# The first feed-forward of a decoder layer, rebuilt in two phases with seven block products

## The chip, the cores and the metric

The kernel runs on one core of a Trainium2 chip. The core has a matrix engine (TensorE, PE in the profile; its weight loads are PEld), three engines for elementwise work (VectorE or DVE, ScalarE or ACT, GpSimd or POOL), a SyncE (SP) that only issues transfers, and 16 DMA engines that move data between DRAM and the on-chip memory SBUF. Matmul results land in PSUM banks, from which DVE or ACT fetch them. Each engine runs its own instructions in order and waits for the others by semaphores.

The metric is the device time of one execution in microseconds (us), lower is better. A difference of about 0.3% is what a measurement of this kernel can tell from none.

## The reference

One decoder layer on a sequence of 1024 tokens of width 1024, in float32: a half-weighted feed-forward, a mixer (attention heads beside state-space heads), cross-attention on 256 memory tokens, and a second half-weighted feed-forward, each between two root-mean-square norms.

```python
def swiglu(h, w_gu, w_down):
    gu = h @ w_gu                      # 1024 x 5632
    g, u = jnp.split(gu, 2, axis=-1)   # two of 2816
    return (jax.nn.silu(g) * u) @ w_down

def reference(x, mem, ...):
    h = x
    f = swiglu(rmsnorm(h, ffn1_pre_g), ffn1_w_gu, ffn1_w_down)
    h = h + 0.5 * rmsnorm(f, ffn1_post_g)
    m = hybrid_mixer(rmsnorm(h, mix_pre_g), w_in, ..., w_out)
    h = h + rmsnorm(m, mix_post_g)
    c = memory_cross_attention(rmsnorm(h, xa_pre_g), rmsnorm(mem, mem_g), xa_wq, xa_wkv, xa_wo)
    h = h + rmsnorm(c, xa_post_g)
    f = swiglu(rmsnorm(h, ffn2_pre_g), ffn2_w_gu, ffn2_w_down)
    return h + 0.5 * rmsnorm(f, ffn2_post_g)
```

The change touches the first feed-forward, and what is prepared during it for later stages.

## The kernel before

**Numbers.** A float32 matrix is written as a high and a low part in the engine's fast float format: `split` (lines 245 to 249) casts the high part on ACT and subtracts it from the source on DVE (or on POOL, if asked). A product is then three matmuls: high by high, high by low, low by high (`mm3`, line 264).

**Tiling.** Activations lie transposed, 128 features by 512 tokens to a tile: 8 depth tiles for each half of the sequence (`XH`, `XL`; hh is 0 or 1). A gate or up weight tile is 128 output columns by 8 depths (512 KB). One projection of one weight tile and one half is 8 x 3 = 24 matmuls of 512 columns (`proj`, line 271). The inner width of 2816 gives 22 hidden tiles, each with a gate weight and an up weight.

**Order of work.** PE's order is written out by hand: each matmul is chained to the one before it, and a clock adds a modelled cost for each (0.422 ns a column, line 130). Work for other engines that should happen beside the matmuls is put on a list with a due time on that clock (`self.later`) and is issued when the clock gets there (`run_later`).

**First feed-forward** (`ffn1`, line 579). For each hidden tile it projects gate and up for both halves; DVE applies the norm's row (line 588), ACT the silu, DVE multiplies in the up result (line 593), and the product is split into high and low on ACT and POOL and kept in SBUF (line 596). After each two hidden tiles follow their down products (`down`, line 470): 96 matmuls into the `dn` banks, added into 16 running sums F by DVE (line 499). At the end, half 0 gets its last down products first; then its norm and residual (`post`, line 378) run beside half 1's last gate, up and down products. Half 1's norm runs beside the start of the state-space stage (`ssd`).

**Prepared weights** (`prepare`, line 185; `prepare_all`, line 226). During the first feed-forward, 82 weight tiles of later stages are loaded, split on ACT and DVE, and written back to DRAM as high and low parts: 20 of the state-space stage, 24 of attention, 16 of the mixer's output ("out"), 8 query and 8 output weights of cross-attention ("q", "o"), and 6 of the second feed-forward. One half of a tile is one step, due every 3500 on the clock from 40000. A stage takes a weight by `wtile` (line 169): a prepared one as two loads of 512 KB, another as one load of 512 KB and a split on the spot. `wstream` keeps one weight ahead.

**Second feed-forward** (`ffn2`, line 655), in two phases. `up_phase` (line 689) does the first three hidden tiles plainly (PLAIN). For the other 19 it sees the weights and the inputs as 2 x 2 blocks (depth halves by gate and up; depth halves by sequence halves) and needs seven block products of 12 matmuls instead of eight (`seven`, line 805). For this it makes sums of input blocks (S1, S4, S5, and differences that overwrite parts of XH and XL; `combine`, line 722), sums of weight blocks on POOL (line 773), and combines the results on DVE, ACT and POOL. Hidden results go to DRAM (`store`, line 701). `down_phase` (line 861) then loads them again, together with the down weights, three loads ahead.

Of the kernel before, what the change touches and what calls it, by code (L numbers as in the profile page):

```python
# [46 lines left out]
class Kern:  # L47
# [137 lines left out]
    def prepare(self, tiles, sp, t0, step):  # L185

# [275 lines left out]
    def dtile(self, src):  # L462
        raw = self.t(self.dp, [P, H], F32, "draw", bufs=2)
        self.nc.sync.dma_start(out=raw, in_=src)
        wh = self.t(self.dp, [P, H], F32R, "dhi", bufs=4)
        wl = self.t(self.dp, [P, H], F32R, "dlo", bufs=4)
        self.split(wh, wl, raw)
        return wh, wl

    def down(self, blocks, halves, first):  # L470


        for dh in range(2):
            ws = [self.dtile(src[dh, k]) for src, _ in blocks for k in range(2)]
            for hh in halves:
                ps = [self.t(self.dnp, [P, H], F32, "dn", bufs=4) for _ in range(4)]
                for j, w in enumerate(ws):
                    for i in range(4):
                        self.down_mm(ps[i], w, blocks[j // 2][1][(j % 2, hh)], i, hh, j == 0, j == len(ws) - 1)
                        if j == len(ws) - 1:  # L480
                            self.down_sum(self.F[hh][self.fi(dh, i, hh)], ps[i], first)

# [93 lines left out]
    def new_F(self):  # L576
        self.F = [[self.t(self.fp, [P, H], F32, f"F{hh}{d}") for d in range(KT)] for hh in range(2)]

    def ffn1(self, wgu, wdn, gpost, gnext, begin):
        nc = self.nc  # L580
        with self.pools("ff", ["a"], ["f"]) as (sp, fp, dnp):
            self.fp, self.dp, self.dnp, self.rows = fp, fp, dnp, False
            self.new_F()
            NB = NFF // 2

            def gate(ps, hh):
                t = self.t(sp, [P, H], F32, "ft", bufs=2)
                nc.vector.tensor_tensor(out=t, in0=ps, in1=self.R[hh], op=ALU.mult)  # L588
                nc.scalar.activation(t, t, AF.Silu)
                return t  # L590

            def up(t, ps):
                nc.vector.tensor_tensor(out=t, in0=t, in1=ps, op=ALU.mult)  # L593
                hi = self.t(sp, [P, H], F32R, "hhi", bufs=7)
                lo = self.t(sp, [P, H], F32R, "hlo", bufs=7)
                self.split(hi, lo, t, nc.gpsimd)
                return hi, lo

            def one(f, hh, act):
                t = gate(self.proj_now(next(W), hh), hh)  # L600
                act[(f, hh)] = up(t, self.proj_now(next(W), hh))

            def both(f, act):
                w = next(W)
                ts = [gate(self.proj_now(w, hh), hh) for hh in range(2)]
                w = next(W)
                for hh in range(2):
                    act[(f, hh)] = up(ts[hh], self.proj_now(w, hh))

            idx = list(range(4 * NB))
            idx += idx[-4:]
            W = [wgu[i] for i in idx]
            act = {}
            w = [self.wtile(W[0])]
            begin(0)
            w.append(self.wtile(W[1]))
            begin(1)
            w.append(self.wtile(W[2]))  # L620
            begin(2)
            ts = []
            for hh in range(2):
                t = gate(self.proj_now(w[0], hh), hh)
                act[(0, hh)] = up(t, self.proj_now(w[1], hh))
                ts.append(gate(self.proj_now(w[2], hh), hh))
            self.prepare_all(sp)
            W = self.wstream(W[3:])
            w = next(W)
            for hh in range(2):  # L630
                act[(1, hh)] = up(ts[hh], self.proj_now(w, hh))
            for b in range(1, NB - 1):
                prev, act = act, {}
                both(0, act)
                self.down([(wdn[b - 1], prev)], [0, 1], b == 1)
                both(1, act)
            prev = act
            act = {}
            one(0, 0, act)
            one(1, 0, act)  # L640
            last = [(wdn[NB - 2], prev), (wdn[NB - 1], act)]
            self.resid(0, 2000)
            self.down(last, [0], False)
            self.run_later(float("inf"))
            self.post(0, gpost, self.C[0], gnext, step=1800)
            one(0, 1, act)
            one(1, 1, act)
            self.place(fp, 32)
            self.resid(1, 2000, 6000)
            self.down(last, [1], False)  # L650
            c1 = self.C[1]
            self.flush(0)
            self.post(1, gpost, c1, gnext)

    def ffn2(self, wgu, wdn, gpre, gpost, out):
# [4 lines left out]
        nc, tc = self.nc, self.tc  # L660
        NB = NFF // 2
        with self.pools("f2", ["r"], []) as (rw, dnp):
            self.dnp, self.rows = dnp, True
            act_d = [[tc.dram_tile([P, 2, H], F32, name=f"act{b}{hh}") for hh in range(2)] for b in range(NB)]
            self.banks = self.raws = 0
            plain = [self.wsrc("gu2", i) for i in range(2 * PLAIN)]

            def bank():
                self.banks += 1
                if self.banks % 7 < 3:  # L670
                    return self.t(self.mmp, [P, H], F32, "mm")
                return self.t(dnp, [P, H], F32, "dn", bufs=4)

            def load(src, shape):
                self.raws += 1
                pool, tag = ((self.wp, "wraw"), (rw, "raw2"))[self.raws // 2 % 2]
                raw = self.t(pool, shape, F32, tag, bufs=2)
                nc.sync.dma_start(out=raw, in_=src)
                return raw

            with tc.tile_pool(name=self.nm("up"), bufs=1, reuse_waits="tile") as sp, \
                    tc.tile_pool(name=self.nm("ub"), bufs=1, reuse_waits="tile") as sp2:
                self.up_phase(sp, sp2, wgu, gpre, act_d, bank, load, plain)
            with tc.tile_pool(name=self.nm("dl"), bufs=1, reuse_waits="tile") as sp, \
                    tc.tile_pool(name=self.nm("dr"), bufs=1, reuse_waits="tile", side="right") as fp:
                self.fp, self.ep = fp, sp
                self.down_phase(sp, wdn, act_d, bank, load, gpost, out)

    def up_phase(self, sp, sp2, wgu, gpre, act_d, bank, load, plain):
        nc = self.nc  # L690

        fts, es = [self.t(sp, [P, H], F32, "ft", bufs=4)], [self.t(sp, [P, H], F32, "e")]
        S = {n: [self.t(sp, [P, 2, H], F32R, f"S{n}{k}") for k in range(4)] for n in (1, 4, 5)}
        S = {n: [(x[:, 0], x[:, 1]) for x in v] for n, v in S.items()}
# [3 lines left out]
        def ft():  # L698
            return fts.pop() if fts else self.t(sp, [P, H], F32, "ft", bufs=4)
# [14 lines left out]
        def tiles(n, src):  # L714
            tmp[n] = self.t(sp2, [P, 2, H], F32, "blk", bufs=5)
            for i, (hh, d) in enumerate(src):
                self.kp(nc.gpsimd.dma_start(out=tmp[n][:, i], in_=self.h[hh][d]))
# [4 lines left out]
        def combine(dst, x, d, y, op):  # L722

            u = self.t(sp, [P, 4, P], F32, "wc", bufs=3).rearrange("p a b -> p (a b)")
# [24 lines left out]

        def again(k):  # L750
# [11 lines left out]
        def pieces(f):  # L762
# [4 lines left out]
            for a, b, op in (  # L767
# [3 lines left out]
                if b is not None:  # L771
                    t = self.t(sp, [P, 4, P], F32, "wc", bufs=3)
                    nc.gpsimd.tensor_tensor(out=t, in0=a, in1=b, op=op)
                    a = t
                n = self.nblk = (self.nblk + 1) % 11
# [1280 lines left out]
```

## Time and profile before

| What | Value |
|---|---|
| median of 3 runs | 2861.12 us |
| lowest, highest run | 2856.28, 2863.88 us |
| the profiled execution, its own time | 2858.9 us |
| mean granted TensorE clock of the profiled execution | 0.981 |

The profile is of one execution. Its span runs from the first to the last instruction and is 1.8 us shorter than that execution's time; all stretches below are counted from the start of the span. By the instructions in the trace, the first feed-forward's products end at 750 us, the state-space stage follows to about 1128, attention to about 1733, the mixer's output to about 1905, cross-attention to about 2155, and the second feed-forward to the end.

In a row of a stretch stand the busy times of the engines, the clock that PE was granted, and the share of time in which the DMA engines were at work. In a row of a group stand the line, the engine, the operation, what it writes and reads, how often, the busy time and the mean length of one, and the idle time of the engine just before them with what ended it.

### The profile page before, as it was taken

The numbers are of one execution on the slowest core, as the hardware profiler recorded it, in microseconds if no ns is written. First come the engines' busy times: TensorE is split into PE (matmuls) and PEld (weight loads), VectorE is DVE, ScalarE is ACT, GpSimd is POOL, SyncE is SP. The second block draws the span as 40 slices with busy tenths as digits, with TensorE's granted clock in tenths as the row PEclk, the third lists the DMA queues.
The fourth block names the chain that finished last, engine by engine and source line by source line (L and its number), as shares of the span: only waits on it lengthen the run. The fifth ranks groups of instructions, "written<-read, shape, count | busy, mean of one in ns | idle before, by whom it ended". The sixth has DMA issues, their size and how long they took to land.

```text
span 2857.1 us, 36755 instructions
## 1 busy us (share of the span) xinstructions
PE 2748.1 (96%) x13194; PEld 2249.0 (79%) x13194; DVE 1769.7 (62%) x2590; ACT 1242.7 (43%) x2213; POOL 716.3 (25%) x862
## 2 busy tenths in 40 slices
PE   8999999999899999999999899999999999999998
PEld 7888888888677778888888787787777688888887
DVE  5555555556766565778777885636255855555657
ACT  6333333334444454566666663324344433332223
POOL 2010000002513343000000042432123655543322
PEclk9999999999899999999999999999999999999999
DMA  5788777876422224343333437666457322224332
GB/s 186 252 271 272 260 258 268 264 252 207 166 89 74 74 72 153 113 115 101 89 90 96 130 123 271 230 219 208 173 206 260 127 75 88 89 81 140 129 132 101
DMA packets 195734, 464.63 MB, mean 163 GB/s; under 512 B 23520, under 2 KB 32608, under 8 KB 195552
## 3 DMA queue, kind: packets, MB, share of 16 engines
q1 hardware_dynamic: 105184, 277.70, 29.8%
q10 hardware_dynamic: 77184, 140.54, 14.6%
q0 software_dynamic: 13184, 44.05, 4.4%
q8 instruction: 104, 1.70, 0.2%
q14 instruction: 78, 0.64, 0.1%
HBM read 314.35 MB, written 126.88 MB: 154 GB/s over the span
## 4 chain that ended last, share of the span: by engine, by line
PE 82%; DVE 8%; ACT 4%; issue 3%; DMA 2%; POOL 1%; SPq 0%; DVEq 0%; ACTq 0%; POOLq 0%
PE mm L133 50%; PE dn L133 24%; DVE nb L1468 2%; PE z L133 2%; PE tr L136 1%; PE ms L133 1%; DVE be L1472 1%; PE ms L136 1%; PE y L133 1%; ACT nb L1463 1%; PE seg L133 1%; DMA wlo<-dwlo 1%; ACT be L1463 1%; DVE acc L359 1%; DVE xl L256 1%
## 5 line engine op out<-in xcount | busy, mean ns | idle before, releaser
L133 PE MATMUL mm<-xh,whi 128*128 128x512 f32 x1776 | 720.5, 408 | 19.3 <-ACT xh L253 8.8
L133 PE MATMUL mm<-xl,whi 128*128 128x512 f32 (+1 forms) x1768 | 697.5, 395 | 3.6 <-DVE xl L256 2.0
L133 PE MATMUL mm<-xh,wlo 128*128 128x512 f32 x1768 | 694.2, 395 | 0.0
L133 PEld LDWEIGHTS mm<-xh,whi 128*128 128x128 f32 x1776 | 338.9, 191 | 84.2 <-ACT xh L253 9.6
L133 PEld LDWEIGHTS mm<-xh,wlo 128*128 128x128 f32 x1768 | 336.3, 190 | 75.1 <-issue 1.4
L133 PEld LDWEIGHTS mm<-xl,whi 128*128 128x128 f32 x1768 | 337.8, 191 | 60.8 <-DVE xl L256 3.7
L248 POOL TENSOR_TENSOR hlo<-ft,hhi 128x512 fp32r<-128x512 f32 x44 | 68.7, 1561 | 580.5 <-ACT hhi L246 580.5
L1468 DVE TENSOR_TENSOR_SCAN nb<-nb,begin 128x128 f32<-128x128 f32 (+7 forms) x128 | 176.4, 1381 | 33.6 <-ACT nb L1463 33.6
L499 DVE TENSOR_TENSOR F<-F,dn 128x512 f32<-128x512 f32 (+1 forms) x221 | 146.3, 682 | 78.1 <-PE dn L133 78.1
L133 PE MATMUL dn<-hhi,dhi 128*128 128x512 f32 x352 | 138.5, 393 | 3.9 <-DVE F L499 3.9
L133 PE MATMUL dn<-hlo,dhi 128*128 128x512 f32 x352 | 138.8, 394 | 0.0
L133 PE MATMUL dn<-hhi,dlo 128*128 128x512 f32 x352 | 138.3, 393 | 0.0
L1463 ACT ACTIVATE nb<-z,scale 128x128 f32<-128x128 f32 (+2 forms) x192 | 111.8, 582 | 41.9 <-PE z L133 40.1
L246 ACT CAST whi<-wraw 128x1024 fp32r<-128x1024 f32 (+1 forms) x83 | 78.8, 950 | 77.3 <-PE dn L133 30.9
L1463 ACT ACTIVATE be<-z,scale 128x128 f32<-128x128 f32 (+2 forms) x192 | 111.1, 579 | 0.0
L1472 DVE TENSOR_TENSOR be<-be,nb 128x128 f32<-128x128 f32 (+7 forms) x128 | 103.8, 813 | 11.5 <-DVE nb L1468 0.5
L1467 POOL MEMSET nb<- 128x1 f32 x128 | 12.7, 99 | 385.0 <-DVE be L1472 362.6
L359 POOL TENSOR_TENSOR acc<-acc,sq 128x512 f32<-128x512 f32 x45 | 62.3, 1384 | 144.8 <-ACT sq L357 144.7
L588 DVE TENSOR_TENSOR ft<-mm,rpre 128x512 f32<-128x512 f32 x44 | 30.4, 691 | 98.3 <-PE mm L133 96.4
L359 DVE TENSOR_TENSOR acc<-acc,sq 128x512 f32<-128x512 f32 x45 | 45.4, 1009 | 72.0 <-ACT sq L357 71.5
L133 PE MATMUL mm<-ath,v 128*128 128x256 f32 x320 | 87.9, 297 | 1.9 <-ACT sq L1483 1.9
L593 DVE TENSOR_TENSOR ft<-ft,mm 128x512 f32<-128x512 f32 x44 | 30.3, 688 | 93.0 <-PE mm L133 90.9
(485 smaller groups left out, 6082.6 us busy)
## 6 DMA issues: line engine op xcount, KB each, us to landing
whi<-dwhi SPq DMA_DIRECT2D x124, 512.0 KB, 3.4
wlo<-dwlo SPq DMA_DIRECT2D x124, 512.0 KB, 4.5
wraw<-in_w_gu SPq DMA_DIRECT2D x67, 512.0 KB, 4.5
dwhi<-acc ACTq DMA_DIRECT2D x55, 256.0 KB, 4.0
dwlo<-acc ACTq DMA_DIRECT2D x55, 256.0 KB, 3.6
dwhi<-rpost ACTq DMA_DIRECT2D x55, 256.0 KB, 4.0
dwlo<-dg ACTq DMA_DIRECT2D x55, 256.0 KB, 3.8
dwhi<-sq ACTq DMA_DIRECT2D x54, 256.0 KB, 3.6
```

Of the source, the lines that this page charges most:

```text
L133: self._pe(self.nc.tensor.matmul(out, lhsT, rhs, start=start, stop=stop, skip_group_check=self.more), cost)
L136: self._pe(self.nc.tensor.transpose(out, src, self.ident if ident is None else ident), 109.0)
L246: self.kp(self.nc.scalar.copy(hi, src))
L248: (eng or self.nc.vector).tensor_tensor(out=lo, in0=src, in1=hi.bitcast(F32), op=ALU.subtract)
L256: self.nc.vector.scalar_tensor_tensor(out=lo, in0=src, scalar=g, in1=hi.bitcast(F32), op0=ALU.mult, op1=ALU.subtract)
L359: self.kp(eng.tensor_tensor(out=accs[i % 2], in0=accs[i % 2], in1=sq, op=ALU.add))
L499: self.nc.vector.tensor_tensor(out=F, in0=F, in1=ps, op=ALU.add)
L588: nc.vector.tensor_tensor(out=t, in0=ps, in1=self.R[hh], op=ALU.mult)
L593: nc.vector.tensor_tensor(out=t, in0=t, in1=ps, op=ALU.mult)
L1463: nc.scalar.activation(o[:, s0:s1], z[:, 0:n], AF.Sigmoid, scale=sc[:, k, i : i + 1])
L1468: nc.vector.tensor_tensor_scan(out=nb[:, 0:Wd][:, ::-1], data0=nb[:, 0:Wd][:, ::-1], data1=begin[:, S - Wd : S][:, ::-1], initial=0.0, op0 ...
L1472: nc.vector.tensor_tensor(out=be[:, 0:Wd], in0=be[:, 0:Wd], in1=nb[:, 1 : Wd + 1], op=ALU.mult)
```

## The change

The first feed-forward now uses the code of the second. `ffn1` calls `up_phase` and `down_phase`; its old loop, `down` and `dtile` are gone.

- `up_phase` gets its buffer counts as a parameter (results, weight sums and blocks: 3, 2, 3 for the first feed-forward, 4, 3, 5 for the second as before) and a path for the first (`begin`): the start of the kernel (loading and norm of x) runs inside it, six gate and up weights are used plainly for both halves, and input blocks are loaded again from x and summed at other due times than in the second: three sums for each of four depth tiles from 19000 on, the lower-left block (`below`) during half 1's plain products, the upper-right one (`last`) from the first block product on.
- `down_phase` gets a path for the first feed-forward: no output rows, all products of half 1 as ordinary down products, the norm of half 0 beside them and that of half 1 after them.
- `prepare_all` prepares 58 tiles: "out" 0 to 7, "q" and "o" are left out, so that `wtile` splits these when they are used. Steps are due every 4050 from 70000. Loads and stores of the preparing are issued on SP's queue, not ACT's, and its third pair of buffers is new.
- In the state-space stage some buffers move to the other side of SBUF.

```diff
@@ prepare, prepare_all
-        pools = ((self.fp, "acc0"), (self.fp, "acc1")), ((self.fp, "rpost"), (self.tp, "dg")), ((self.tp, "sq0"), (self.tp, "sq1"))
+        pools = ((self.fp, "acc0"), (self.fp, "acc1")), ((self.fp, "rpost"), (self.tp, "dg")), ((sp, "bh"), (sp, "bl"))
...
-            self.kp(nc.scalar.dma_start(out=raws[n], in_=work[n][0][:, work[n][2], :]))
+            self.kp(nc.sync.dma_start(out=raws[n], in_=work[n][0][:, work[n][2], :]))
...
-                self.kp(nc.scalar.dma_start(out=d[:, work[n][2], :].bitcast(F32), in_=x.bitcast(F32)))
+                self.kp(nc.sync.dma_start(out=d[:, work[n][2], :].bitcast(F32), in_=x.bitcast(F32)))
...
-        names += [("out", i) for i in range(16)] + [("q", i) for i in range(8)] + [("o", i) for i in range(8)]
-        names += [("gu2", i) for i in range(2 * PLAIN)]
-        self.ready = dict(zip(names, self.prepare([ap["w_" + n][i] for n, i in names], sp, 40000, 3500)))
+        names += [("out", i) for i in range(8, 16)] + [("gu2", i) for i in range(2 * PLAIN)]
+        self.ready = dict(zip(names, self.prepare([ap["w_" + n][i] for n, i in names], sp, 70000, 4050)))
@@ ffn1 (the old one, with down and dtile, is removed)
+    def ffn1(self, wgu, wdn, gpre, gpost, gnext, begin):
+        tc = self.tc
+        with self.pools("ff", [], ["r"]) as (rw, dnp):
+            self.fp, self.rows = rw, False
+            act_d, bank, load = self.ffn(dnp, rw)
+            with tc.tile_pool(name=self.nm("up"), bufs=1, reuse_waits="tile") as sp, \
+                    tc.tile_pool(name=self.nm("ub"), bufs=1, reuse_waits="tile") as sp2:
+                self.up_phase(sp, sp2, wgu, gpre, act_d, bank, load, None, (3, 2, 3), rw, begin)
+            with tc.tile_pool(name=self.nm("dl"), bufs=1, reuse_waits="tile") as sp, \
+                    tc.tile_pool(name=self.nm("d1"), bufs=1, reuse_waits="tile", side="right") as f1, \
+                    tc.tile_pool(name=self.nm("d0"), bufs=1, reuse_waits="tile", side="right") as f0:
+                self.new_F(f0, f1)
+                self.down_phase(sp, wdn, act_d, bank, load, gpost, None, gnext)
@@ up_phase
+        T0 = self.clock
+        if begin:
+            x = sums(F32)
+            self.F = [[x[(1, 4)[hh]][d // 2][:, d % 2] for d in range(KT)] for hh in range(2)]
+            first = []
+            for i in range(3):
+                first.append(self.wtile(wgu[i]))
+                begin(i)
...
+        def below(k):
+            c, a = (tmp["ca", k][:, i] for i in range(2))
+            scale(a, k)
+            combine(B21[k], c, k + 4, a, ALU.subtract)
...
-        t0 = T0 + 27000
+        t0, dt = (T0 + 12000, 7000) if begin else (T0 + 27000, 8000)
+        early = [("ad", k) for k in range(4)] + [("ca", k) for k in range(2)] if begin else []
         for k in range(4):
-            at(t0 + 8000 * k, fetch, k)
-            for n, f in enumerate(steps(k)):
-                at(t0 + 8000 * (k + 1) + 1500 * n, f)
+            at(t0 + dt * k, fetch, k)
+            for n, f in enumerate(steps(k)[: 4 if begin else 5]):
+                at(t0 + dt * (k + 1) + 1500 * n, f)
...
+        if begin:
+            ts = []
+            for hh in range(2):
+                up(0, hh, gate(first[0], hh), first[1])
+                ts.append(gate(first[2], hh))
+            self.prepare_all(rw)
+            W = self.wstream([wgu[i] for i in range(3, 2 * PLAIN)])
+            ws = []
+            for k, t in enumerate((27000, 33500, 34000, 34500)):
+                at(t0 + t, tiles, ("ca", k), [(0, k + 4), (0, k)])
+            for hh in range(2):
+                if hh:
+                    for k in range(4):
+                        at(self.clock + 1000 + 3500 * k, below, k)
+                        if k < 3:
+                            at(self.clock + 12500 + 500 * k, again, k)
+                t = ts[hh]
+                for i in range(2 * PLAIN - 3):
+                    if not hh:
+                        ws.append(next(W))
+                    if i % 2:
+                        t = gate(ws[i], hh)
+                    else:
+                        up(1 + i // 2, hh, t, ws[i])
...
         for k in range(4):
-            at(self.clock + 1500 * k, again, k)
-            at(self.clock + 1500 * k + 5000, last, k)
+            if k == 3 or not begin:
+                at(self.clock + (200 if begin else 1500 * k), again, k)
+            at(self.clock + 1500 * k + (0 if begin else 5000), last, k)
         for f in range(PLAIN, NFF):
             seven(f)
@@ down_phase
-                x = place() if b == 0 else self.t(sp, [P, 2, H], F32R, "hl", bufs=8)
+                x = place() if b == 0 else self.t(sp, [P, 2, H], F32R, "hl", bufs=8 if out else 6)
...
+        if not out:
+            self.resid(0, 2500)
         for hh in range(2):
             for bs in pairs:
...
-                    if not hh or bs is pairs[0]:
+                    if not out or not hh or bs is pairs[0]:
                         group(ws[dh], xs, dh, hh, False)
             if hh == 0:
                 self.run_later(float("inf"))
-                self.post(0, gpost, self.C[0], out=out[0], step=1800)
+                self.post(0, gpost, self.C[0], gnext, out=out and out[0], step=1800)
+                if not out:
+                    self.resid(1, 2000, 6000)
+        if not out:
+            c1 = self.C[1]
+            self.flush(0)
+            self.post(1, gpost, c1, gnext)
+            return
@@ ssd (the tiles "xs" and "Ct" only)
-                out = self.t(sp, [P, S], F32, tag, bufs=bufs)
+                out = self.t(sp if tag == "Bt" else ep, [P, S], F32, tag, bufs=bufs)
```

More of the change, by code (lines that the diff above doesn't have):

```diff
@@ L459, in pre @@
         self.R[hh], self.C[hh] = r, c
[L462 to L481, printed above, removed]
     def fi(self, dh, i, hh):
@@ L574, in last_rows @@
         finish(3, shift(3), 256)
[L576 to L679, printed above, removed]
+    def new_F(self, *pools):
+        self.F = [[self.t(fp, [P, H], F32, f"F{hh}{d}") for d in range(KT)] for hh, fp in enumerate(pools)]
@@ L778, in pieces @@
                 else:
[L779 removed]
+                    w = self.t(sp2, [P, 2, 4, P], F32R, "blk", bufs=NBLK)
                 self.split(w[:, 0], w[:, 1], a)
@@ L847, in up_phase, with gate @@
[L847 to L853 removed]
+            at(t0 + dt * k, fetch, k)
+            for n, f in enumerate(steps(k)[: 4 if begin else 5]):
+                at(t0 + dt * (k + 1) + 1500 * n, f)
+        def gate(w, hh):
+            t = ft()
+            scaled(t, self.proj_now(w, hh), hh)
+            return t
@@ new lines, in up @@
+        def up(f, hh, t, w):
+            ps = self.proj_now(w, hh)
+            nc.vector.tensor_tensor(out=t, in0=t, in1=ps, op=ALU.mult)
+            store(f, hh, t)
+        if begin:
[20 more added lines that the diff above has]
+                        t = gate(ws[i], hh)
+                    else:
+                        up(1 + i // 2, hh, t, ws[i])
+        else:
+            W = self.wstream(plain + plain)
+            for hh in range(2):
+                for f in range(PLAIN):
+                    t = gate(next(W), hh)
+                    up(f, hh, t, next(W))
```

83 lines of the change are left out of this document (51 added, 32 removed).

## The prediction

> **What bounds the kernel now.** I read the page first: the engines' busy shares and the chain that ended last, by engine. Then came the busy times by stretch, the chain in order of time, PE's waits, and the groups by line.
>
> ```profile
> span 2857.1 us, 36755 instructions
> PE 2748.1 (96%) x13194; PEld 2249.0 (79%) x13194; DVE 1769.7 (62%) x2590; ACT 1242.7 (43%) x2213; POOL 716.3 (25%) x862
> PE 82%; DVE 8%; ACT 4%; issue 3%; DMA 2%; POOL 1%; SPq 0%; DVEq 0%; ACTq 0%; POOLq 0%
> ```
>
> TensorE ends 82% of the chain. A share is a mean over stages, so the stretches matter more. Their columns are the stretch, its length, then busy us and instructions of PE, PEld, DVE, ACT and POOL, the granted clock, the DMA share and GB/s.
>
> ```profile
> 0.00:45.56 45.56, 36.55 (x151) 28.79 (x152) 31.39 (x42) 34.28 (x53) 10.74 (x15) 1.00 0.60 203
> 45.56:668.75 623.19, 623.19 (x2750) 515.98 (x2750) 340.83 (x466) 213.43 (x323) 62.59 (x40) 1.00 0.78 258
> 668.75:750.00 81.25, 73.55 (x305) 58.51 (x304) 52.54 (x71) 37.01 (x59) 32.86 (x38) 0.92 0.49 165
> 750.00:850.00 100.00, 92.03 (x396) 69.36 (x395) 70.37 (x107) 41.47 (x63) 23.59 (x21) 0.91 0.32 116
> 1765.00:1905.00 140.00, 134.44 (x577) 108.07 (x576) 67.76 (x89) 37.25 (x63) 60.65 (x61) 0.98 0.66 237
> 1905.00:2160.00 255.00, 242.96 (x1166) 198.35 (x1164) 112.72 (x261) 104.39 (x215) 51.29 (x65) 0.99 0.57 200
> 2225.00:2260.00 35.00, 28.00 (x96) 19.80 (x95) 30.47 (x37) 18.37 (x32) 24.06 (x21) 0.85 0.39 126
> 2317.21:2450.49 133.28, 133.28 (x590) 110.36 (x589) 75.55 (x105) 46.14 (x77) 68.34 (x50) 1.00 0.26 83
> 2583.77:2800.00 216.23, 216.23 (x956) 179.04 (x955) 128.18 (x191) 60.02 (x103) 68.98 (x62) 1.00 0.41 136
> ```
>
> The first feed-forward ends its products at 750 us. From 45.56 to 668.75 PE has no idle time and the full clock, so there only fewer matmuls give time. Its ends (0 to 45.56, 668.75 to 850) lose time to other engines. The last three rows are the second feed-forward, which already has the form that the first is to get: its step from plain to block products (2225 to 2260), block products (2317 to 2450), and down products. The last two have no idle PE either.
>
> **The change part by part.** *Matmuls removed.* In the chain in order of time (start, us, what):
>
> ```profile
> 81.40 21.76 PE dn L133 x96
> 103.16 43.52 PE mm L133 x192
> 2317.21 19.04 PE dn L133 x84
> ```
>
> A 512-column matmul costs 21.76/96 = 0.2267 us in either form. For one hidden tile, gate and up are 2 weights x 2 halves x 8 depths x 3 = 96 matmuls; seven block products are 7 x 4 x 3 = 84. Three tiles stay plain, so 19 change: 19 x 12 = 228 matmuls, **-51.7 us**. The down products keep their 1056.
>
> *Is the block stretch still PE's?* It repeats every 7 tiles, 133.28 us. Per tile of 19.04 us that is DVE 10.8, ACT 6.6, POOL 9.8. Preparing weights now runs beside it. The clock charges 0.422 ns a column, 216 ns for 0.2267 us, so a step of 4050 lasts 4.25 us: 4.48 steps a tile.
>
> ```profile
> L211 DVE TENSOR_TENSOR sq<-xl,sq 128x512 fp32r<-128x512 f32 x27 | 21.8, 806 | 5.2 <-ACT sq L206 3.0 <-DMA dwlo<-sq 2.2
> L206 ACT CAST rpost<-braw 128x512 fp32r<-128x512 f32 x7 | 4.3, 621 | 11.8 <-DVE sq L211 4.3 <-DMA dwhi<-rpost 3.3 <-DMA xl<-in_w_qkv 1.9
> ```
>
> Each step adds a subtract (0.81) and a cast (0.62): DVE 10.8 + 3.6 = 14.4, ACT 9.4, POOL 9.8, all under 19.04. DMA: 768 KB a step is 185 GB/s, with the block form's 83 it is 268, against 258 carried now. Loads and stores of the preparing move to SP's queue; a store held by its subtract holds the next gate and up weights behind it, but those are asked for a tile (19 us) ahead. I cost this at **0**. If the cover goes, each microsecond of lateness per tile costs 19 us.
>
> *Results by DRAM.* Stores go on ACT's queue; the loads of down follow three ahead on SP's. Down takes tile 0 first, and the last tile's result only some 170 us later (768 matmuls). The second feed-forward does the same with no idle PE (its last row): **0**.
>
> *The step from plain to block products.* New here is a stretch in which inputs are summed and split on ACT and DVE. Its likeness in the second feed-forward held 96 matmuls in 35 us, 21.8 us at full pace: 13.2 us lost. PE's waits there (engine, line <- releaser: us, times, longest):
>
> ```profile
> PE mm L133 <- DVE xl L248: 2.0, 4, 0.8
> PE mm L133 <- DVE whi L248: 1.9, 1, 1.9
> PE mm L133 <- ACT xh L246: 1.9, 2, 1.3
> PE mm L133 <- ACT whi L246: 1.0, 1, 1.0
> ```
>
> DVE was 30.47 of 35 us busy: sums, weight splits and the last input block (lines 726 to 756) stood in one queue, behind a norm. The change spreads them: twelve sums early, the lower-left block during the second half's plain products, only the last block at the step. Twelve sums are 24 operations of about 0.69 us, 17 us of DVE, into a stretch with 45% of DVE free. But the first block weights still wait behind the last plain product's evacuation. Bounds 0 to +13.2; I take about half, **+6**. POOL's 32 added input loads fit: it is busy 10.74 of the first 45.56 us.
>
> The Trainium skill (TensorE: Matmul & The Clock Gate, Why this matters for your kernels) says that the clock halves after PE gaps over about 3 us. By it the waits above, each under 2 us, would leave the clock alone and the step would cost 6.8 us. The row of 2225 disagrees: its granted clock was 0.85.
>
> *The tail.* Before, 288 large matmuls (65.3 us) took 81.25: 16.0 lost. In the groups of that stretch:
>
> ```profile
> L133 PE MATMUL dn<-hhi,dhi 128*128 128x512 f32 x63 | 26.1, 414 | 3.9 <-DVE F L499 3.9
> L133 PE MATMUL ms<-small,acc 128*128 128x1 f32 x16 | 2.9, 304 | 3.8 <-DVE acc L361 3.8
> ```
>
> After, the norm of half 0 lies beside 192 down matmuls of half 1, as many as now, with loads three ahead. The second wait is the norm's own chain and stays; the first may go, as down products without a norm beside them show no idle PE. Against it, more sums (16 for 8) and weight splits share DVE. Bounds -8 to +8; I take **-3**.
>
> *Tiles no longer prepared.* 24 weights (out 0 to 7, q, o) are now split where they are used: 16 loads in the mixer's output (1765 to 1905) and 32 in cross-attention (1905 to 2160).
>
> ```profile
> L248 DVE TENSOR_TENSOR wlo<-wraw,whi 128x1024 fp32r<-128x1024 f32 x56 | 72.4, 1292 | 15.8 <-ACT whi L246 15.6
> L246 ACT CAST whi<-wraw 128x1024 fp32r<-128x1024 f32 x64 | 66.9, 1047 | 27.8 <-PE mm L133 11.6 <-DMA wraw<-in_w_gu 9.7 <-DVE ft L588 3.5
> 1920.00:1950.00 30.00, 26.17 (x128) 21.51 (x127) 27.03 (x53) 17.83 (x38) 12.30 (x15) 0.94 0.53 181
> 2070.00:2100.00 30.00, 27.59 (x142) 23.04 (x141) 23.18 (x56) 17.74 (x42) 9.47 (x12) 0.94 0.61 201
> PE dn L133 <- DMA wlo<-dwlo: 1.1, 2, 0.7
> ```
>
> 48 x 1.29 = 62 us of DVE and 50 of ACT. DVE is busy 68 of 140 and 113 of 255 us, so most hides. The two stretches of 30 us above are where norms already crowd DVE. At 32 tiles in 255 us each gets 3.8 tiles, 4.9 us: the first then asks 31.9 of 30, the second 28.1. I count 2 us over, 3 for what queues behind a cast in order, and -1 for the DMA wait that half the bytes spare: **+4**. Bounds: -4 (shorter loads alone) to +62 (nothing hidden).
>
> *Moved buffers* of the state-space stage and the start of the kernel (same loads, same six plain products): **0**, within 4 either way, since half 1's norm crowds DVE from 750 to 850 as before.
>
> Sum: -51.7 + 6 - 3 + 4 = -44.7. The profiled execution took 2858.9 us: 2814.2. The median is 2.2 above it: **2816**.
>
> **The rivals.** *The edges help:* the step costs nothing, the tail loses its 7.7 us of waits, and the raw weights spare their DMA wait: -51.7 - 7.7 - 1 = -60, 2801. For it: the sums are moved early. Against it: DVE is 31.39 of 45.56 us busy at the start already.
>
> *The raw weights show:* half of their 62 us of DVE lands on the path: -51.7 + 6 - 3 + 31 = -18, 2843. For it: in cross-attention PE waits are for DVE (softmax, norms). Against it: DVE is under half busy there.
>
> *DVE and POOL exclude each other* in the block stretch, and it turns **slower**. In one window of block products:
>
> ```profile
> L248 DVE TENSOR_TENSOR blk<-wc,blk 128x512 fp32r<-128x512 f32 x17 | 15.6, 920 | 5.1 <-ACT blk L246 5.0
> L248 DVE TENSOR_TENSOR blk<-raw,blk 128x512 fp32r<-128x512 f32 x4 | 2.8, 688 | 5.5 <-ACT blk L246 5.5
> L773 POOL TENSOR_TENSOR wc<-wraw,raw 128x512 f32<-128x512 f32 x11 | 14.2, 1293 | 8.8 <-DVE blk L248 4.8 <-DVE whi L248 2.4 <-DVE wlo L248 1.7
> ```
>
> The same subtract takes 0.69 or 0.92 us, the longer where POOL's sums run. If DVE stood still during each POOL operation, a tile would need 7 x 1.29 for POOL and (15 + 4.5) x 0.69 for DVE, 22.5 us against 19.04: 3.4 x 19 = +65, in all +21, 2882. It decides once the two together pass 21.4 us a tile (44.7/19 over 19.04). Against it: in the row of 2317 DVE and POOL are busy 143.9 of 133.28 us, so they do overlap.
>
> The Trainium skill (SBUF — State Buffer, Who interferes with whom) has the rule for this: a VectorE operation with two SBUF inputs and a GpSimd one lock each other out. By it alone 8 + 4.5 such operations and POOL's seven ask 17.7 of 19.04 us, which still fits; the rows agree in direction.
>
> *The matmuls do not fall:* PE's count on the page would stay near 13194 rather than drop by 228; the code leaves no room for it.
>
> **How the numbers follow.** Forecast (2802 to 2832) 0.67; edges help 0.12; raw weights show 0.12, most of it still clearly faster; exclusion 0.05 in full; the rest, 0.04, exclusion in part, ends near no change. This kernel's runs can tell about 0.3%, 8.6 us. Faster 0.91, same 0.04, slower 0.05. The range takes the good edges and the raw-weight case and leaves the exclusion out: 2797 to 2845.
>
> **What would show it.** PE's count falls to about 12966; pieces of 19.04 us with 84 matmuls repeat from about 87 to 449 us without idle PE; the first feed-forward ends near 701 us, not 750; the step loses under 13 us; cross-attention is up to 5 us longer. I am wrong if PE idles within the block stretch, if DVE is over 95% busy there, or if 1765 to 2160 grows by more than 15 us.

## The result and the profile after

The changed kernel takes 2888.28 us (median of 4 runs, 2887.47 to 2889.92) beside 2858.70 for the kernel before (4 runs): ratio 1.0104, 95% interval [1.0082, 1.0126]. It is slower by 1.0%, where 2816 us was forecast. The rival in which DVE and POOL exclude each other comes near by number (2882), but not by its mechanism: it has TensorE idle in the block products, and there TensorE has no gap.

The page of the changed kernel, its span, busy times and chain by engine:

```profile
span 2888.1 us, 37031 instructions
...
PE 2707.2 (94%) x12966; PEld 2211.7 (77%) x12966; DVE 1971.1 (68%) x2789; ACT 1329.9 (46%) x2384; POOL 941.5 (33%) x1027
...
PE 74%; DVE 11%; ACT 5%; DMA 4%; issue 4%; POOL 2%; SPq 0%; DVEq 0%; ACTq 0%; POOLq 0%
```

The matmuls fell by 228, from 13194 to 12966, as worked out. Yet TensorE's part of the chain fell from 82% to 74%: what its missing work would have given, and more, went to waits. Where, the stretches of the same trace say (stretch, length, then busy us and instructions of PE, PEld, DVE, ACT, POOL, the granted clock, DMA share, GB/s):

```profile
45.56:160.00 114.44, 100.73 (x420) 81.55 (x421) 91.69 (x117) 58.40 (x99) 56.55 (x52) 0.94 0.71 235
160.00:440.00 280.00, 280.00 (x1237) 231.93 (x1236) 234.09 (x286) 127.74 (x227) 161.45 (x102) 1.00 0.79 265
440.00:500.00 60.00, 56.53 (x246) 45.55 (x244) 42.19 (x61) 21.23 (x37) 15.95 (x11) 1.00 0.81 280
500.00:550.00 50.00, 7.98 (x28) 6.38 (x28) 20.17 (x29) 16.56 (x28) 3.83 (x3) 0.59 1.00 372
550.00:700.00 150.00, 150.00 (x663) 124.20 (x663) 93.96 (x136) 39.89 (x69) 41.47 (x37) 1.00 0.39 130
```

The block products (160 to 440) run without a gap, as forecast. From 500 to 550 TensorE works 8 of 50 us, at a DMA share of 1.00. PE's waits in the trace after (engine, line <- releaser: us, times, longest), first from 460 to 560, then from 0 to 160, then from 680 to 860:

```profile
PE dn L133 <- ACT whi L244: 42.0, 1, 42.0
...
PE mm L133 <- DVE e L760: 7.3, 1, 7.3
...
PE mm L133 <- ACT whi L244: 4.9, 1, 4.9
...
PE ms L133 <- DVE acc L359: 18.2, 4, 12.8
```

So there are three places: one wait of 42.0 us early in the down products, the step from plain to block products, and the tail with the norm's small matmuls ("ms"). The releaser of the first is a cast of a down weight on ACT; but ACT is busy 16.56 of 50 us. The chain in order of time says what held the weight:

```profile
506.20 5.09 DMA dwhi<-rpost
...
512.03 5.08 DMA dwhi<-rpost
...
517.86 5.08 DMA dwhi<-rpost
...
523.68 5.20 DMA dwhi<-rpost
...
530.37 4.85 DMA dwlo<-dg
...
536.05 0.32 SPq L214
...
536.43 4.88 DMA raw<-in_w_dn
...
541.39 0.63 ACT whi L244
...
542.06 7.48 PE dn L133 x24
```

These are stores of *prepared weights of later stages* (line 214), one waiting for a buffer of the one before; the down weight that TensorE waits for is loaded only after the last of them. SP's own timeline (start, length) has them in one queue:

```profile
462.99 0.32 SPq L574 DMA_DIRECT2D wraw<-act  x1
463.55 0.32 SPq L214 DMA_DIRECT2D dwlo<-dg  x1
...
536.05 0.32 SPq L214 DMA_DIRECT2D dwlo<-dg  x1
536.43 0.45 SPq L574 DMA_DIRECT2D raw<-in_w_dn  x1
```

Between the two loads of line 574 (what the down products need) at 462.99 and 536.43 SP issues nothing but preparing. Seven of these loads had gone out from 423.07 on; the eighth stands behind all of it. In the code `up_phase` ends with `self.run_later(float("inf"))`, line 835: it empties the list of due work, whatever its due time. The 116 steps of preparing are due up to 70 + 115 x 4.05 = 536 us on the planner's clock. On the same clock the plain and block products end near 407 (288 + 19 x 84 = 1884 matmuls of 0.216), so the steps left, more than a quarter of them, are issued at once, ahead of most loads of `down_phase`.

To see how much each part of the first feed-forward costs, here is the first VectorE operation of the state-space stage, in the trace before and in the trace after:

```profile
752.25 0.72 DVE L953 CAST side<-params 128x128 fp32r<-128x128 f32 x1
```

```profile
778.82 0.72 DVE L939 CAST side<-params 128x128 fp32r<-128x128 f32 x1
```

The first feed-forward is 26.6 us longer, where -48.7 was forecast (-51.7 + 6 - 3). The remaining stages add 31.0 - 26.6 = 4.4 us of the span's 31.0, near the +4 forecast for them. The error is all in the first feed-forward.

### The profile page after: what moved, and what is told of

It reads as the page before. It is cut to its first block, busy times and chain, and to the rows that moved or that the text cites. A ratio compares the mean times of both kernels' runs of the same rounds, so it can differ in the third digit from the quotient of the medians.

```text
span 2888.1 us, 37031 instructions
## 1 busy us (share of the span) xinstructions
PE 2707.2 (94%) x12966; PEld 2211.7 (77%) x12966; DVE 1971.1 (68%) x2789; ACT 1329.9 (46%) x2384; POOL 941.5 (33%) x1027
## 2 busy tenths in 40 slices
DMA packets 180251, 433.19 MB, mean 150 GB/s; under 512 B 21600, under 2 KB 30688, under 8 KB 180064
## 4 chain that ended last, share of the span: by engine, by line
PE 74%; DVE 11%; ACT 5%; DMA 4%; issue 4%; POOL 2%; SPq 0%; DVEq 0%; ACTq 0%; POOLq 0%
PE mm L133 41%; PE dn L133 26%; DVE nb L1455 2%; PE z L133 2%; PE tr L136 1%; PE ms L133 1%; DVE be L1459 1%; PE ms L136 1%; PE y L133 1%; DMA dwhi<-rpost 1%; ACT nb L1450 1%; PE seg L133 1%; DVE acc L357 1%; DMA blk<-in_xT 1%; DVE xl L254 1%
## 5 line engine op out<-in xcount | busy, mean ns | idle before, releaser
L133 PE MATMUL mm<-xh,whi 128*128 128x512 f32 x1280 | 523.1, 418 | 24.4 <-ACT xh L251 8.9
L133 PE MATMUL mm<-xl,whi 128*128 128x512 f32 (+1 forms) x1216 | 484.3, 398 | 2.3 <-DVE xl L246 1.6
L133 PE MATMUL mm<-xh,wlo 128*128 128x512 f32 x1240 | 484.1, 398 | 0.0
L133 PEld LDWEIGHTS mm<-xh,whi 128*128 128x128 f32 x1280 | 247.0, 193 | 70.4 <-ACT xh L251 9.7
L133 PEld LDWEIGHTS mm<-xh,wlo 128*128 128x128 f32 x1240 | 237.3, 191 | 54.9 <-issue 1.5
L133 PEld LDWEIGHTS mm<-xl,whi 128*128 128x128 f32 x1216 | 234.6, 193 | 39.2 <-DVE xl L246 3.0
L246 DVE TENSOR_TENSOR wlo<-wraw,whi 128x1024 fp32r<-128x1024 f32 x62 | 83.9, 1354 | 59.9 <-ACT whi L244 54.6
L476 DVE TENSOR_TENSOR F<-F,dn 128x512 f32<-128x512 f32 x150 | 98.1, 679 | 35.4 <-PE dn L133 35.4
L714 POOL TENSOR_TENSOR wc<-wraw,raw 128x512 f32<-128x512 f32 x58 | 83.3, 1437 | 54.0 <-DVE blk L246 18.3
L133 PE MATMUL dn<-xh,blk 128*128 128x512 f32 x312 | 100.8, 389 | 0.0
```

Of the source, the lines that this page charges most:

```text
L133: self._pe(self.nc.tensor.matmul(out, lhsT, rhs, start=start, stop=stop, skip_group_check=self.more), cost)
L246: (eng or self.nc.vector).tensor_tensor(out=lo, in0=src, in1=hi.bitcast(F32), op=ALU.subtract)
L476: self.nc.vector.tensor_tensor(out=F, in0=F, in1=ps, op=ALU.add)
```

## The experiments

Theories ahead of the runs: F, the emptied list (line 835) costs the 42 us; S, the step costs more than forecast since preparing starts in it; T, at the tail the next norm's small matmuls stand in TensorE's queue before VectorE has made their input. Rivals: the DMA volume is too much wherever it is issued; the raw weights cost it; the waits are the new form's own.

**e1_no_flush.** The list keeps steps that are due later than 6 us ahead.

```diff
-        self.run_later(float("inf"))
+        self.run_later(self.clock + 6000 if begin else float("inf"))
```

> Edit: at the end of the first feed-forward's block products only work due within 6000 is issued, not the whole list. Theory F (flush): there the changed kernel empties its list of due work, which puts the 34 steps of preparing that are left (34 x 512 KB of stores, 30 x 256 KB of loads, 25.7 MB, 64 us at the 402 GB/s that the trace shows) in front of down's first loads on SP's queue; PE waits 42.0 us and restarts at half clock. Without it that wait is gone and the steps run beside the down products: 2888 falls by 40 to 46, to about 2845, and PE has no wait over 3 us between 480 and 560. Rival V (volume): the 25.7 MB and their casts and subtracts collide with down's loads or with the norm of half 0, and half or more comes back between 500 and 780: 2865 or more.

Measured: 2846.96 us, ratio 0.9968 [0.9955, 0.9981], 41 us less than the changed kernel. One line turns slower into faster. Its stretches, then SP's timeline:

```profile
45.56:160.00 114.44, 100.48 (x419) 80.83 (x418) 91.61 (x117) 59.05 (x100) 55.97 (x52) 0.94 0.68 236
...
500.00:550.00 50.00, 49.16 (x216) 40.01 (x215) 37.43 (x54) 17.76 (x32) 13.14 (x9) 1.00 0.81 280
```

```profile
463.88 0.32 SPq L574 DMA_DIRECT2D wraw<-act  x1
464.43 0.32 SPq L214 DMA_DIRECT2D dwlo<-dg  x1
...
469.30 0.32 SPq L214 DMA_DIRECT2D dwhi<-acc  x1
475.19 0.38 SPq L574 DMA_DIRECT2D raw<-in_w_dn  x1
```

The same preparing and the loads of down now alternate, and TensorE has 49.16 of 50 us. F is shown; the order costs, not the bytes: the same kernel moves 433.18 MB in all (after: 433.19). The step still has 419 matmuls.

**e2_late_norm.** The changed kernel, with the next norm's two sums for half 0 due 8 us later; the list is still emptied.

```diff
+            wait = 12000 if step == 1800 else 4000
-            q.append((t + t1 + 4000, lambda: self.rms_cols([accs2], c2)))
+            q.append((t + t1 + wait, lambda: self.rms_cols([accs2], c2)))
...
-                q.append((t + t2 + 4000, lambda: self.rms_rows(c2[:, :], r2_)))
+                q.append((t + t2 + wait, lambda: self.rms_rows(c2[:, :], r2_)))
```

> Edit: in the first feed-forward the sums for half 0's next norm are due 8000 later in PE's order, behind the last down product of half 1; the flush stays. Theory T (tail): in the changed kernel PE stands 12.8 us at these sums (763.3 us) while down products that could run are behind them, because DVE's chain of the norm now takes 56 us from half 0's last product and not 46; then the clock is at 0.5. Moved behind them, 10 to 15 us are gained: about 2876. Rival: the norm is needed next anyway, by the state-space stage's first evacuation, and the wait moves there: 2888 within 4.

Measured: 2879.20 us (4 runs, 2874.64 to 2884.16), ratio 1.0081 [1.0060, 1.0102], 9 us less than the changed kernel, where 10 to 15 were expected. PE's waits from 680 to 860:

```profile
PE ms L133 <- DVE acc L359: 8.5, 3, 4.4
```

The wait of 12.8 us shrinks to 4.4 (18.2 to 8.5 in all). T holds: the down products behind the small matmuls had been ready, in a queue that is worked in order. The rival doesn't: TensorE's wait at the start of the state-space stage stays as it was (4.4 us, 4.5 in the changed kernel).

**e4_before_58.** The kernel before, with the shorter list of prepared tiles alone.

```diff
-        names += [("out", i) for i in range(16)] + [("q", i) for i in range(8)] + [("o", i) for i in range(8)]
-        names += [("gu2", i) for i in range(2 * PLAIN)]
+        names += [("out", i) for i in range(8, 16)] + [("gu2", i) for i in range(2 * PLAIN)]
```

> Edit: the kernel before, with 58 weights prepared instead of 82, nothing else. It measures the cost of splitting 24 weights (48 loads) where they are used. By the prediction: 4 us slower than before (2859 to about 2863), all of it between the end of attention and the end of cross-attention. By the traces of before and after, those two stages together took about 5 us longer. Rival raw weights: 15 us or more slower. Other rival: no cost or a gain, since the first feed-forward carries less: 2859 or less.

Measured: 2861.29 us, ratio 1.0013 [1.0002, 1.0023], 4 us more. The stretches of the mixer's output and of cross-attention, which stand in the prediction for the kernel before:

```profile
1765.00:1905.00 140.00, 133.09 (x573) 107.23 (x571) 92.72 (x101) 50.49 (x75) 67.63 (x62) 0.98 0.50 176
1905.00:2160.00 255.00, 242.48 (x1153) 198.19 (x1154) 145.46 (x290) 130.02 (x244) 52.49 (x65) 0.97 0.41 140
```

VectorE takes on 25.0 and 32.7 us (62 forecast), and TensorE keeps nearly its busy time: it is nearly all hidden. The raw weights are not the cause.

**e5_flush_on_act.** The changed kernel, with loads and stores of the preparing on ACT's queue, as before the change (lines 200 and 214).

```diff
-            self.kp(nc.sync.dma_start(out=raws[n], in_=work[n][0][:, work[n][2], :]))
+            self.kp(nc.scalar.dma_start(out=raws[n], in_=work[n][0][:, work[n][2], :]))
...
-                self.kp(nc.sync.dma_start(out=d[:, work[n][2], :].bitcast(F32), in_=x.bitcast(F32)))
+                self.kp(nc.scalar.dma_start(out=d[:, work[n][2], :].bitcast(F32), in_=x.bitcast(F32)))
```

> Edit: the changed kernel with the loads and stores of the preparing on ACT's queue, as before the change; the flush stays. If it is SP's order alone that holds down's loads (theory F in its narrow form), down's loads no longer stand behind them and the wait of 42 us shrinks to under 15: about 2860. If the flush holds through ACT and DVE too (down's casts and subtracts stand behind the preparing's, which wait for stores), PE still waits 30 us or more there: 2880 to 2895.

Measured: 2926.60 us, ratio 1.0250 [1.0229, 1.0271]: worse by another 38 us. PE's longest wait from 400 to 600, and a part of the chain:

```profile
PE mm L133 <- ACT whi L244: 81.3, 1, 81.3
```

```profile
475.56 4.59 DMA dwhi<-acc
480.23 0.45 ACT acc L205
480.68 4.47 DMA dwhi<-bh
```

Now SP is free and issues its loads of down, the last two before the wait at 455.81 and 456.36 us. But their casts are ACT instructions, and ACT now stands in order through the same preparing, up to 549.94 us: a store lands, its buffer is cast again, the next store follows. So F fails in its narrow form (SP's order alone), and holds in its wider one, though the time is above what that gave (2880 to 2895). The queue that is flooded is not the point; that something needed at once stands behind the flood is.

**e3_prep_late.** e1_no_flush, with the preparing begun 25 us later and a little faster.

```diff
-        self.ready = dict(zip(names, self.prepare([ap["w_" + n][i] for n, i in names], sp, 70000, 4050)))
+        self.ready = dict(zip(names, self.prepare([ap["w_" + n][i] for n, i in names], sp, 95000, 3800)))
```

> Edit: as e1 (no flush), and the preparing starts at 95000 with a step of 3800 on the clock instead of 70000 and 4050. It asks what the step from plain to block products costs and why. In e1 the stretch from 45.56 to 160 us holds 419 matmuls, 95.0 us of 114.4 (19.4 lost): PE waits 4.4 us for the first block weight, then 7.3 and 1.2 us near 121 to 131 for DVE, which is busy 10 of 10 us there, and the clock drops after each. Theory S (preparing at the step): the subtracts and stores of the preparing stand in DVE's and ACT's queues while the block weights catch up; without them the waits of 7.3 and 1.2 and half of the lost clock go: 8 to 12 us less than e1's 2847, about 2837. Rival: the block weights' own subtracts beside POOL's sums fill DVE (1.75 us each there, not 0.69) and the wait stays: 2847 within 3.

Measured: 2836.56 us, ratio 0.9921 [0.9902, 0.9940], 10 us less than e1_no_flush. The step's stretch:

```profile
45.56:160.00 114.44, 104.94 (x441) 84.28 (x440) 89.46 (x114) 56.32 (x94) 54.88 (x53) 0.97 0.57 196
```

S holds for a part: 22 matmuls more in the stretch, 5.0 us, and the wait of 7.3 us (DVE e) shrinks to 0.9. The other 5 us of the gain lie behind this stretch. The step still does 441 matmuls where the kernel before did 506.

**e6_all_three.** e3_prep_late and the later norm of e2_late_norm.

> Edit: e3 (no flush, preparing later) and e2's move of half 0's next norm behind half 1's last down products. If the three losses are separate, the gains add: e1's 2847, less 8 to 12 for the step, less 9 for the tail (e2 against the changed kernel): 2826 to 2830, 1% under the kernel before. If the tail's wait is one of DVE's backlog that moves to the state-space stage, 2833 to 2838.

Measured: 2831.67 us, ratio 0.9903 [0.9884, 0.9923]: the best of all, 1% below the kernel before and 57 us below the changed one. The later norm gives 5 us here, not 9. Its state-space stage starts here:

```profile
721.06 1.28 DVE L940 CAST side<-params 128x128 fp32r<-128x128 f32 x1
```

**e8_all_82.** e6_all_three, with all 82 tiles prepared again, a step every 2.8 us.

```diff
-        names += [("out", i) for i in range(8, 16)] + [("gu2", i) for i in range(2 * PLAIN)]
-        self.ready = dict(zip(names, self.prepare([ap["w_" + n][i] for n, i in names], sp, 95000, 3800)))
+        names += [("out", i) for i in range(16)] + [("q", i) for i in range(8)] + [("o", i) for i in range(8)]
+        names += [("gu2", i) for i in range(2 * PLAIN)]
+        self.ready = dict(zip(names, self.prepare([ap["w_" + n][i] for n, i in names], sp, 95000, 2800)))
```

> Edit: e6 with all 82 weights prepared again, in steps of 2800 instead of 3800. Theory: the 24 left-out weights cost about 4 us where they are used (e4 against before: 2861.3 against 2856.9), and the block stretch carries 82: DVE 10.8 + 6.5 x 0.81 = 16.0 of 19.04 us a tile, DMA 83 + 267 = 350 GB/s. Then 2822 to 2826. Rival (exclusion of DVE and POOL, or DMA at its limit): PE waits within the block stretch, over 1 us a tile, 19 us or more: 2845 or more.

Measured: 2861.21 us, ratio 1.0007 [0.9994, 1.0020], 30 us more than e6_all_three and near its rival (2845 or more). The block products' stretch, first of e6_all_three, then of e8_all_82:

```profile
160.00:440.00 280.00, 280.00 (x1236) 231.56 (x1235) 237.86 (x293) 131.90 (x235) 162.29 (x102) 1.00 0.84 286
```

```profile
160.00:440.00 280.00, 267.71 (x1159) 217.51 (x1158) 244.85 (x298) 135.95 (x243) 150.37 (x97) 0.99 0.94 333
```

Here the cover of the block products ends: at a step every 2.8 us the DMA engines are at 0.94, VectorE at 87%, and TensorE does 77 matmuls fewer (17.5 us). TensorE's waits there are all for VectorE's sums (line 762: 12.3 us in 12 waits), and VectorE itself stands 9.5 us for stores of the preparing, which it never does in e6_all_three. How much is VectorE's own load and how much the DMA engines' this pair doesn't separate. So at this pace preparing only 58 tiles is not a loss of 4 us but what makes room for the block form; 82 tiles at a slower pace were not tried.

**e7_loads_on_sp** and **e9_stores_on_pool** ask what is left of the step. e7 is e6_all_three with the later reloads of input blocks on SP's queue; e9 adds the stores of results on POOL's queue.

```diff
-                self.kp(nc.gpsimd.dma_start(out=tmp[n][:, i], in_=self.h[hh][d]))
+                self.kp((nc.sync if begin and n not in early else nc.gpsimd).dma_start(out=tmp[n][:, i], in_=self.h[hh][d]))
@@ e9 only
-            self.later.append((self.clock + 4500, lambda: self.kp(nc.scalar.dma_start(out=o, in_=t))))
+            self.later.append((self.clock + 4500, lambda: self.kp((nc.gpsimd if begin else nc.scalar).dma_start(out=o, in_=t))))
```

> The three edits together (e6_all_three), and the later reloads of input blocks issued on SP's queue instead of POOL's. Question: what is the 4.7 us wait of TensorE for the first block weight (ACT whi) at 84.5 us? Theory Q: POOL's queue is held 8.0 us by a reload that waits for a buffer (POOL blk <- DVE wc), and the sum of weights of the first block product stands behind it. Then that wait falls from 4.7 to under 2.5 us, the clock after the gap stays above its 0.79, and the time falls by 3 to 6 us against e6_all_three: ratio to before 0.988 to 0.989 (e6: 0.9903). Rival: the split on ACT waits for ACT's own scaling of the reloads, which wait 3 to 8 us for their DMA; the wait stays above 4 us and the time within 2 us of e6_all_three (0.990).

> e7_loads_on_sp, and the stores of hidden results in the first feed-forward issued on POOL's queue instead of ACT's. In e6_all_three ACT's queue stands 2.8 us at 120.9 us because a store waits for POOL's product (ACT sq <- POOL ft 3.69), and the eviction of a block product behind it leaves TensorE idle about 2.3 us at a clock of 0.83 in 120 to 130. Theory: that gap goes, 2 to 5 us less than e7_loads_on_sp. Rival: POOL, busy 162 of 280 us in the block stretch, is held by 44 more issues of about 0.5 us (22 us) and its sums come late: no change or a few us slower, with TensorE waits for POOL or for whi in the block stretch.

Measured: 2831.45 us (0.9907 [0.9891, 0.9923]) and 2836.15 us (0.9923 [0.9910, 0.9937]); the theories of both fell. In e7_loads_on_sp PE's waits from 0 to 160, and the first sum of weights on POOL:

```profile
PE mm L133 <- ACT whi L244: 4.9, 1, 4.9
PE mm L133 <- DVE e L761: 4.0, 1, 4.0
```

```profile
87.31 1.26 POOL L715 TENSOR_TENSOR wc<-wraw 128x512 f32<-128x512 f32 x1 [10.07 <-DVE xl L246]
```

POOL stands idle 10.07 us, free of reloads, and the sum starts hardly earlier than before (87.68 in e6_all_three). It waits for VectorE to finish with an input sum: both kinds of sums use the buffer "wc", of which the first feed-forward has two. So the first block weight stands behind the input sums, whose reloads land 3.0 to 10.2 us after their issue (in e6_all_three). The rival of e7 had the wait and the time right, but the cast on ACT waits for POOL's sum, not for ACT's own scaling. A third buffer was not tried; the gap stays open as to its price. In e9_stores_on_pool the gap between 120 and 132 us stays too: 0.7 us for ACT and 3.2 for VectorE, 4.0 for VectorE in e7_loads_on_sp, 2.3 and 0.9 in e6_all_three. So the store that waited on ACT's queue was not what made it. The 5 us that e9 is slower are what its rival allowed, but the intervals overlap, and its trace is of its fastest run (2830.86 us), so where they lie is open.

## Why the prediction was wrong

**Right:** the matmuls (-51.7; the count is exact), the block products without idle PE, the raw weights (+4 forecast; e4_before_58 3.7 by its ratio). None of the three signs that were to prove it wrong came up: no idle PE in the block stretch, VectorE at 84% there (not 76%, but under 95%), and 4.4 us more behind the first feed-forward. They stood where the prediction had looked. The subtract of a step, forecast at 0.81 us, is longer beside POOL's sums; in the groups of 160 to 440 in the trace after:

```profile
L210 DVE TENSOR_TENSOR acc<-xl,acc 128x512 fp32r<-128x512 f32 x12 | 15.9, 1322 | 0.0
...
L210 DVE TENSOR_TENSOR dg<-xl,rpost 128x512 fp32r<-128x512 f32 x11 | 9.7, 881 | 0.0
```

The exclusion rival leant the right way but didn't decide in the block products, for TensorE has 280.00 of 280 us there. It has a part at the step before them (below).

**The step that failed: "Results by DRAM ... 0".** The prediction took the loads of down to be "three ahead on SP's", and the second feed-forward as witness. But that one prepares no weights. The prediction itself had said that the preparing moved to SP's queue, "a store held by its subtract holds the next gate and up weights behind it", and looked at this only within the block products. It never asked where the steps end: by the numbers in the diff, at 536 us of the planner's clock (562 us on the chip, by its own 4.25 us for a step of 4.05), past the end of the block products that it had put near 449 us. Line 835 did the rest. Worth +41 (e1_no_flush).

**"The step from plain to block products", mis-sized:** +6 with a bound of 13.2. Measured in the stretch 45.56 to 160 as 506 - 420 = 86 matmuls of 0.2267 us: +19.5. The row of the kernel before:

```profile
45.56:160.00 114.44, 114.44 (x506) 94.73 (x506) 59.25 (x81) 39.34 (x59) 14.66 (x9) 1.00 0.72 237
```

The likeness in the second feed-forward had no preparing beside it; beginning it later and at a quicker pace gives 10 us back in all. Exclusion adds to it: in the trace after, VectorE works without a break from 112 us to the sum "e" at 130.78 us, for which TensorE waits 7.3 us, and eight of its subtracts on the way took 1.18 to 1.78 us instead of 0.68, 8.1 us in all (the last section shows why). No run separates this from the preparing. The rest is input sums ahead of the first block weight and a slower clock behind gaps. In e6_all_three, PE's waits from 0 to 160, and the 10 us behind that wait:

```profile
PE mm L133 <- ACT whi L244: 4.7, 1, 4.7
```

```profile
90.00:100.00 10.00, 10.00 (x36) 7.97 (x36) 7.91 (x12) 6.60 (x13) 5.52 (x7) 0.79 0.38 135
```

TensorE is busy throughout, but with 36 matmuls where 44 fit: 0.79 of the clock. The Trainium skill (TensorE: Matmul & The Clock Gate, Why this matters for your kernels) puts the loss of the full clock at gaps over about 3 us; these rows agree. Others don't. In the same trace a gap of 2.35 us, ending at 124.31, was enough (0.50 from 126 to 128 us):

```profile
120.00:130.00 10.00, 6.76 (x22) 4.81 (x21) 6.97 (x9) 4.19 (x8) 7.33 (x5) 0.83 0.41 152
```

In e9_stores_on_pool one of 3.21 us, ending at 131.94, was not (1.00 from 120 to 140 us). So here the length of one gap doesn't tell whether the clock falls.

**"The tail", -3 with a bound of +8:** the step, the emptied list and the matmuls account for -51.7 + 19.5 + 41 = 8.8 of the 26.6 us, so some +18 is left for the tail. "The second wait is the norm's own chain and stays" was wrong: the wait of the small matmuls grew to 18.2 us, from this before (680 to 860):

```profile
PE ms L133 <- DVE acc L361: 5.8, 4, 3.5
```

TensorE comes to the small matmuls of the next norm some 43 us after half 0's last product in both traces, but VectorE has their input after 56 us, where it had it after 46. The added sums and weight splits in its queue are the likely reason; that was argued, not tested. It is no echo of the emptied list: in e1_no_flush the wait is 17.5 us. e2_late_norm shows about 9 us of it; in e6_all_three the tail is down to about 721.06 - 752.25 + 51.7 - 14.3 = +6 (63 matmuls are missing from its step, 14.3 us).

e6_all_three lies 16 us above the forecast; these two account for about that: 8 from the step (14.3 for 6) and 9 from the tail (+6 for -3).

## What to carry to other kernels

When due work is moved onto a queue, or its schedule changed, work out when its last step is due and what empties the list before that: everything left is issued there in one go, ahead of what the next phase needs next. A stage that ran clean elsewhere is a witness only if the same background work ran beside it. A small matmul that waits for a slow engine should be placed where that engine is sure to be done, because ready matmuls behind it wait too.

## What the runs showed of the hardware

In the tail of the changed kernel a VectorE sum, 0.68 us long at the median of eleven, took 4.21 us. VectorE's timeline, then POOL's:

```profile
751.31 4.21 DVE L357 TENSOR_TENSOR acc<-acc,sq 128x512 f32<-128x512 f32 x1
...
757.30 0.68 DVE L357 TENSOR_TENSOR acc<-acc,sq 128x512 f32<-128x512 f32 x1
```

```profile
751.34 0.54 POOL L404 DMA_DIRECT2D h<-F  x1
751.90 1.28 POOL L357 TENSOR_TENSOR acc<-acc,sq 128x512 f32<-128x512 f32 x1
753.11 0.56 POOL L404 DMA_DIRECT2D h<-F  x1
753.69 1.27 POOL L260 TENSOR_TENSOR xl<-dg,xh 128x512 fp32r<-128x512 f32 x1
```

It ends at 755.52, 0.56 us after POOL's second operation, having waited out two of them with DMA issues before and between them. The same mark is seen in the block products (160 to 440 in the trace after). Of the subtracts of lines 210 and 246 that VectorE's timeline lists singly, the 53 that no elementwise operation of POOL overlaps took at most 0.69 us. The 74 that took over 0.75 us each end 0.54 to 0.56 us after the end of such an operation; the other 42 overlap one and are no longer than 0.69. So where a subtract is lengthened, VectorE stands until POOL's operation is done, and then needs 0.55 us. The Trainium skill (SBUF — State Buffer, Who interferes with whom) has this as an exclusive lock on a port that the two engines share; these times agree. New in the first trace is that VectorE did not get in between two of POOL's operations, 0.51 us apart. No run isolates it.
